# SSD mixer of a decoder trunk: decay exponents broadcast into two buffers a group ahead, selections as a job of their own, the state's product between the two diagonal parts

## The chip, the core and the metric

The kernel runs on one core of one Trainium2 chip. The metric is the device time of one execution in microseconds (us). Before the change three runs gave 1081.33, 1083.4 and 1087.55 us, a median of 1083.4.

## What is computed

A decoder trunk of two layers on 256 tokens of width 1024. Each layer is a half feed-forward block, a mixer and another half feed-forward block. The mixer of the first layer is attention, that of the second is a Mamba-2 SSD mixer, and this is the part that the change touches. Its 32 heads of width 64 fall into 4 groups of 8; each group has its own B and C (128 states), and the 256 tokens are two chunks of 128. Cut to what matters, per head of a group:

```
a_cs  = cumsum(dt * a)                               # within a chunk
decay = exp(a_cs[l] - a_cs[s])  for l >= s, else 0
y_diag = (C B^T * decay) @ (x * dt)                  # within a chunk
state  = B^T (x * dt * exp(a_cs[last] - a_cs))       # of the first chunk
y_off  = (C @ state) * exp(a_cs)                     # on the second chunk
y = (y_diag + y_off + d * x) * silu(z)
y = y * rsqrt(mean(y*y over the group) + eps) * norm ; out = y @ w_out
```

## The kernel before, in words

Weights are 128 x 1024 units in float32. `Weights.load` (L67) fetches a unit by the SP queue into one of RAW = 4 buffers, `ahead` (L75) splits it into a high part (cast on ScalarE, L86) and a low part (difference on VectorE, L87), PF = 4 units ahead of the one in use and into NB = 8 pairs of buffers. The projections use three matmuls per product for it: high by high, high by low, low by high (L253 to L255 and L258 to L260).

The mixer is `ssm` (L649). For each group g it projects a pair of columns (B and C of the group), two pairs (the group's x) and one z block, a `chunk` of 48 matmuls. `conv2` (L692) does the convolution and SiLU of a pair. The output projection `proj_out` (L300) follows, with 16 K tiles, four per group: 12 units of 24 matmuls, and then the last four (TAIL), taken together. These 96 matmuls all read `yh` and `yl` of group 3.

Everything else of a group is put between the projection's matmuls by a planner written by hand (L151 to L180). A job is a Python generator; each `yield` ends a step, and its value is a rest in us of the planner's own time before the next step is due. `tick(dt)` is called after every few matmuls: it moves that time on, lists the jobs whose predecessors have ended, in the order of their posting, and runs one step of those among the first WIN = 3 that are due. A job leaves the list only when the step after its last `yield` is asked for. `need(job)` runs all that is left of a job, and of what it depends on, at once.

```
ready = [g for g in bg if not any(d in bg for d in deps[g])]
for g in ready[:WIN]:
    if due[g] <= now[0]:
        step(g)
```

Jobs of the mixer: `dts` (L664) makes dt and the cumulated exponents, writes these to DRAM (`scr`, L680), rests L_DT = 18 and transposes them. `ssd(g)` (L710) is the group's scan. Its first step fetches the exponents of the group's 8 heads back from DRAM, broadcast to all 128 partitions: `sg` ("seg"), two transfers of 512 KB (L714), into a single buffer; GpSimd then fills the upper triangle with -BIG (`affine_select`, L716), and C B^T and B's transpose are made (L721, L722). Then come the transposes of x (L733) with `xd` (L737) and d * x on GpSimd (L738), the 16 exponentials (L746), `xe` (L753), the products of the decay with C B^T (L755), the state (L758) and its copy `sta` (L760), the two diagonal parts (L767, 32 matmuls each, added by VectorE in L769), and last the state's product with C (L772), which L774 and L776 scale and add. The banks for L758, L767 and L772 are two in all (`sbank`), taken in turns.

`gate(g, t)` (L780) multiplies by SiLU of z (L788), squares and sums on ScalarE (L790), takes the reciprocal root on GpSimd (L191, L194), scales on VectorE (L792), rests L_GATE = 7, transposes (L796) and splits into yh and yl (L184, L185). The transposes use the two banks of `tbank`, as do those of x.

What orders it: `ssd(g)` is posted after the pairs of group g with a rest of L_SD = 6, after `dts` and all earlier `ssd`; the two gates of g follow `ssd(g)`. Group g > 1 begins with `need(jobs[g - 2])`; before a z block's SiLU stands `need(*gates[g - 2])`; `before(i)` in the output projection calls `need` for the gates of group i // 4. The framework puts each engine's instructions into a fixed order when the kernel is built; it goes by the written order as the priority and may put an instruction that is ready ahead of one that is not.

Of the kernel before, what the change touches and what calls it, by code (L numbers as in the profile page):

```python
# [8 lines left out]
F32 = mybir.dt.float32  # L9
# [5 lines left out]
P = 128  # L15
# [14 lines left out]
WARM = 6  # L30
CONV = 0
L_HEAD, L_FG, L_SM, L_PT = 7.0, 20.0, 5.0, 2.5
L_DT, L_GATE, L_S0, L_S1, L_S2, L_S3, L_SD = 18.0, 7.0, 2.0, 6.0, 1.0, 2.0, 6.0
WIN = 3


# [66 lines left out]
def tile_trunk(ctx, tc, x, wp, sm, gains, ssm_norm, sinks, dskip, out):  # L103
# [18 lines left out]
    def tbank():  # L122
        return pt.tile([P, 512], F32, tag="tp", name="tp")
# [37 lines left out]
    def post(*gens, delay=0.0, after=()):  # L161
        for g in gens:
            due[g] = now[0] + delay
            deps[g] = after
            bg.append(g)
# [96 lines left out]
    def chunk(nk=2, nu=4):  # L262

        accs = [bank(), bank()]
        n = 1024 // nk
        for j in range(nu):
            wh, wl = W.take()
            for t in range(2):
                ts_ = slice(t * P, (t + 1) * P)
                for i in range(nk):  # L270
                    k = j * nk + i
                    ws = slice(i * n, (i + 1) * n)
                    mm_a(accs[t][:, 0:n], xh[:, k, ts_], xl[:, k, ts_], wh[:, ws], wl[:, ws],
                         k == 0, k == KT - 1)
                tick(1.3)
            W.free()
        return accs
# [371 lines left out]
    def ssm(nj, norm):  # L649
        with ExitStack() as es:  # L650
            sp = es.enter_context(tc.tile_pool(name="ssp", bufs=1, reuse_waits="tile"))
# [55 lines left out]

            y1, ngs = {}, {}

            def ssd(g, xT):  # L710
                hs = slice(g * 8, g * 8 + 8)
                sg = sp.tile([P, 2, 8, P], F32, tag="seg", name="seg", bufs=1)
                for c in range(2):
                    nc.sync.dma_start(sg[:, c], scr[None, hs, c * P : (c + 1) * P].partition_broadcast(P))  # L714
                for c in range(2):
                    G.affine_select(out=sg[:, c], in_=sg[:, c], pattern=[[0, 8], [1, P]],  # L716
                                    compare_op=ALU.is_ge, fill=-BIG, base=0, channel_multiplier=-1)
                b = tbank()
                for c in range(2):
                    cs = slice(c * P, (c + 1) * P)  # L720
                    T.matmul(b[:, cs], BT[:, g, cs], CT[:, g, cs], start=True, stop=True)  # L721
                T.transpose(b[:, 256:384], BT[:, g, 0:P], ident)  # L722
                cb = sp.tile([P, 2, P], F32, tag="cb", name="cb", bufs=2)
                A.copy(cb, b[:, 0:S].rearrange("p (c l) -> p c l", c=2))
                bn = sp.tile([P, P], F32, tag="bn", name="bn", bufs=2)
                A.copy(bn, b[:, 256:384])
                yield L_S0
                yt = sp.tile([P, 2, 8, HD], F32, tag="yb", name="y1", bufs=8)
# [30 lines left out]
                sta = sp.tile([P, 512], F32, tag="sta", name="sta", bufs=1)  # L759
                A.copy(sta, bs)  # L760
                yield L_S3
                for c in range(2):
                    b = sbank()
                    for q in range(8):
                        for e in range(2):
                            es_ = slice(e * 64, e * 64 + 64)
                            T.matmul(b[es_, q * HD : (q + 1) * HD], sg[:, c, q, es_], xd[c][:, q, :],  # L767
                                     start=True, stop=True)
                    V.tensor_tensor(yt[:, c], yt[:, c], b.rearrange("p (n d) -> p n d", n=8), ALU.add)  # L769
                    yield  # L770
                b = sbank()
                T.matmul(b, CT[:, g, P:S], sta, start=True, stop=True)  # L772
                tmp = sp.tile([P, 8, HD], F32, tag="xe", name="tmp", bufs=2)
                V.tensor_tensor(tmp, b.rearrange("p (n d) -> p n d", n=8),  # L774
                                eac[:, hs, None].broadcast_to([P, 8, HD]), ALU.mult)
                V.tensor_tensor(yt[:, 1], yt[:, 1], tmp, ALU.add)  # L776
                y1[g] = yt
                yield

# [27 lines left out]
                    r.append(s_)  # L807
                return r

            jobs, gates = [], []  # L810

            def pair(cts, dsts):
                conv2(pair_t(), cts, dsts)

            for g in range(4):
                if g > 1:
                    need(jobs[g - 2])
                xT = sp.tile([P, 4, S], F32, tag="xsT", name="xsT", bufs=2)
                bc = (16 + g, 20 + g), (BT[:, g, :], CT[:, g, :])
                if g == 0:  # L820

                    a0 = pair_t(True)
                    aj = small_proj(wdt)
                    tick(2.6)
                    a1 = pair_t()
                    need(nj)
                    conv2(a0, *bc)
                    jd = dts(aj)
                    post(jd)
                    conv2(a1, (0, 1), (xT[:, 0, :], xT[:, 1, :]))  # L830
                else:
                    pair(*bc)
                for q in range(2 if g == 0 else 0, 4, 2):
                    pair((g * 4 + q, g * 4 + q + 1), (xT[:, q, :], xT[:, q + 1, :]))
                jobs.append(ssd(g, xT))
                post(jobs[g], delay=L_SD, after=[jd] + jobs[:g])
                az = chunk()
                if g > 1:
                    need(*gates[g - 2])
                sz = silu_z(az)  # L840
                gates.append([gate(g, t, sz[t]) for t in range(2)])
                post(*gates[g], after=[jobs[g]])
# [124 lines left out]
```

## Time and profile before

| | us |
|---|---|
| median of three runs | 1083.4 (1081.33 to 1087.55) |
| the profiled execution | 1074.93 |
| its span | 1073.1 |
| TensorE busy | 1043.1 (97%) |
| VectorE busy | 808.7 (75%) |
| ScalarE busy | 621.0 (58%) |
| GpSimd busy | 99.4 (9%) |

The mixer lies between about 692 and 886 us of the span. The profile names engines PE (TensorE matmul), PEld (its weight load), DVE (VectorE), ACT (ScalarE), POOL (GpSimd) and SP (the queue that issues transfers). A matmul's end is modelled, so its recorded duration can reach into the next one's; where a wait begins and which instruction it is put down to is read from the waits. The granted clock is TensorE's, as a share of 2.4 GHz.

### The profile page before, as it was taken

The page shows a single profiled execution, that of the slowest core. Times are in us where ns is not written, and L with a number is a line of the kernel's source. Part 1 is how long each engine was busy: PE and PEld are TensorE (multiplying, and loading weights), DVE is VectorE, ACT ScalarE, POOL GpSimd, SP SyncE. Part 2 cuts the span into 40 slices and gives each one's busy share as a digit, 9 for nine tenths or more (in the row PEclk, how much of TensorE's full clock was granted, in tenths as well). Part 3 has the DMA queues.
Part 4 walks back from the last instruction along what each step waited for, and adds up shares of the span by engine and source line. Part 5 has one row for each costly group of instructions (what it writes and reads, how often), then busy time and mean ns, then how long its engine had stood idle before and what let it go on. Part 6 is the DMA issues. An engine that isn't in the chain of part 4 may idle for free.

```text
span 1073.1 us, 17287 instructions
## 1 busy us (share of the span) xinstructions
PE 1043.1 (97%) x6538; PEld 919.3 (86%) x6538; DVE 808.7 (75%) x1261; ACT 621.0 (58%) x1099; POOL 99.4 (9%) x117
## 2 busy tenths in 40 slices
PE   6999999997999999999999999999899999999998
PEld 5888888885888888888888888998888998888887
DVE  4898876666788888766888876587889768888751
ACT  5765654555666555454655654478878656555530
POOL 3000001243020000011000001101231121000000
PEclk8999999999999999999999999999999999999999
DMA  6776565534237666665666666534565636666550
GB/s 216 227 238 195 185 190 194 179 138 139 97 94 225 193 191 185 193 193 168 198 189 195 186 189 194 188 107 157 181 223 188 218 118 202 191 197 183 190 177 20
DMA packets 61603, 191.33 MB, mean 178 GB/s; under 512 B 6440, under 2 KB 15952, under 8 KB 61392
## 3 DMA queue, kind: packets, MB, share of 16 engines
q1 hardware_dynamic: 61520, 190.23, 56.5%
q8 instruction: 51, 0.84, 0.3%
q14 instruction: 32, 0.26, 0.1%
HBM read 189.12 MB, written 1.09 MB: 177 GB/s over the span
## 4 chain that ended last, share of the span: by engine, by line
PE 81%; DVE 5%; POOL 4%; ACT 3%; issue 3%; DMA 3%; SPq 0%; POOLq 0%; DVEq 0%; ACTq 0%
PE mm L339 44%; PE mm L340 23%; PE mm L258 3%; PE mm L260 3%; PE mm L259 3%; DMA seg<-scr_a 1%; DVE lo L87 1%; POOL rstd L194 1%; PE mm L253 1%; PE mm L254 1%; PE mm L255 1%; POOL sqa L216 1%; DVE cv L704 1%; ACT hi L86 1%; PE sb L767 1%
## 5 line engine op out<-in xcount | busy, mean ns | idle before, releaser
L86 ACT CAST hi<-raw 128x1024 fp32r<-128x1024 f32 (+1 forms) x350 | 362.6, 1041 | 346.9 <-PE mm L339 274.1
L87 DVE TENSOR_TENSOR lo<-raw,hi 128x1024 fp32r<-128x1024 f32 (+1 forms) x350 | 426.3, 1222 | 146.2 <-ACT hi L86 145.0
L339 PE MATMUL mm<-xhl,hi 128*128 128x512 f32 x1408 | 494.1, 395 | 7.2 <-ACT hi L86 4.9
L340 PE MATMUL mm<-xhl,lo 128*128 128x256 f32 x1408 | 395.9, 281 | 0.0
L339 PEld LDWEIGHTS mm<-xhl,hi 128*128 128x128 f32 x1408 | 265.6, 189 | 67.0 <-ACT hi L86 4.8
L340 PEld LDWEIGHTS mm<-xhl,lo 128*128 128x128 f32 x1408 | 268.3, 191 | 0.3 <-DVE lo L87 0.2
L339 PE MATMUL mm<-ht,hi 128*128 128x512 f32 x704 | 244.2, 392 | 0.0
L340 PE MATMUL mm<-ht,lo 128*128 128x256 f32 x704 | 197.0, 280 | 0.0
L339 PEld LDWEIGHTS mm<-ht,hi 128*128 128x128 f32 x704 | 131.8, 187 | 29.1
L340 PEld LDWEIGHTS mm<-ht,lo 128*128 128x128 f32 x704 | 133.2, 189 | 0.0
L216 POOL TENSOR_TENSOR sqa<-sqa,sqb 128x256 f32<-128x256 f32 x42 | 38.7, 921 | 597.0 <-ACT sqb L214 595.9
L253 PE MATMUL mm<-hi,xhl 128*128 128x512 f32 (+1 forms) x144 | 58.6, 407 | 0.0
L258 PE MATMUL mm<-xhl,hi 128*128 128x256 f32 x192 | 56.5, 294 | 0.0
L254 PE MATMUL mm<-lo,xhl 128*128 128x512 f32 (+1 forms) x144 | 55.5, 386 | 0.0
L255 PE MATMUL mm<-hi,xhl 128*128 128x512 f32 (+1 forms) x144 | 55.1, 383 | 0.0
L259 PE MATMUL mm<-xhl,hi 128*128 128x256 f32 x192 | 54.9, 286 | 0.0
L260 PE MATMUL mm<-xhl,lo 128*128 128x256 f32 x192 | 54.8, 285 | 0.0
L407 DVE SCALAR_TENSOR_TENSOR h<-mm,h 128x256 f32<-128x256 f32 x64 | 26.6, 422 | 36.5 <-PE mm L340 35.8
L206 DVE SCALAR_TENSOR_TENSOR xhl<-h,gn,xhl 128x256 fp32r<-128x256 f32 x48 | 35.8, 768 | 8.2 <-ACT xhl L205 8.2
L370 DVE TENSOR_TENSOR sumg<-sumg,rB 128x256 f32<-128x256 f32 x88 | 37.4, 425 | 4.9 <-ACT rB L237 2.3
L372 DVE TENSOR_TENSOR sumg<-sumg,rB 128x256 f32<-128x256 f32 x88 | 36.9, 419 | 4.4 <-ACT sumg L371 4.4
L377 DVE TENSOR_TENSOR sumu<-sumu,sumg 128x256 f32<-128x256 f32 x88 | 37.4, 425 | 2.6
(192 smaller groups left out, 1246.0 us busy)
## 6 DMA issues: line engine op xcount, KB each, us to landing
raw<-in_wp_dram SPq DMA_DIRECT2D x345, 512.0 KB, 3.6
seg<-scr_a SPq DMA_DIRECT2D x8, 512.0 KB, 7.0
fbc<-scr_f SPq DMA_DIRECT2D x1, 1024.0 KB, 5.7
ng<-in_ssm_norm_dram SPq DMA_DIRECT2D x4, 256.0 KB, 3.6
out_dram<-h SPq DMA_DIRECT2D x8, 128.0 KB, 2.7
h<-in_x_dram SPq DMA_DIRECT2D x3, 256.0 KB, 6.2
raw<-in_wp_dram SPq DMA_DIRECT2D x2, 256.0 KB, 2.7
smt<-in_sm_dram SPq DMA_DIRECT2D x1, 319.5 KB, 4.1
```

Of the source, the lines that this page charges most:

```text
L86: self.nc.scalar.copy(hi[:, cs], w[:, cs])
L87: self.nc.vector.tensor_tensor(lo[:, cs], w[:, cs], hi[:, cs].bitcast(F32), ALU.subtract)
L216: G.tensor_tensor(sqa, sqa, q, ALU.add)
L253: T.matmul(acc, sh, wh, start=start, stop=False)
L254: T.matmul(acc, sh, wl, start=False, stop=False)
L255: T.matmul(acc, sl_, wh, start=False, stop=stop)
L258: T.matmul(acc, wh, mh, start=start, stop=False)
L259: T.matmul(acc, wh, ml, start=False, stop=False)
L260: T.matmul(acc, wl, mh, start=False, stop=stop)
L339: T.matmul(acc, wh, mhl.rearrange("p e c -> p (e c)"), start=start, stop=False)
L340: T.matmul(acc[:, 0:S], wl, mhl[:, 0, :], start=False, stop=stop)
L370: V.tensor_tensor(s_, s_, rn[1], ALU.mult)
```

## The change

The broadcast and the selection leave `ssd` and become a job `seg(g)`: the first step issues the two transfers, rests L_SG = 9, the second does the two selections. `seg` has two buffers instead of one; `cb` and `bn` have one instead of two. `load_seg` posts the job of the next group: group 0's right after `dts`, group 1's after the z block of group 0 and after `dts` alone, group 2's after the first pair of group 1 and after `ssd(0)`, group 3's after the first pair of group 2 and after `ssd(0)` and `ssd(1)`. `ssd(g)` is now posted after `seg(g)` too. Within `ssd` the state's product moves between the two diagonal parts, with a rest of L_S4 = 2 on either side of it; before, the steps there followed each other without a rest.

```diff
--- before.py
+++ after.py
@@ -30,7 +30,7 @@
 WARM = 6
 CONV = 0
 L_HEAD, L_FG, L_SM, L_PT = 7.0, 20.0, 5.0, 2.5
-L_DT, L_GATE, L_S0, L_S1, L_S2, L_S3, L_SD = 18.0, 7.0, 2.0, 6.0, 1.0, 2.0, 6.0
+L_DT, L_GATE, L_S0, L_S1, L_S2, L_S3, L_S4, L_SD, L_SG = 18.0, 7.0, 2.0, 6.0, 1.0, 2.0, 2.0, 6.0, 9.0
 WIN = 3
 
 
@@ -707,22 +707,31 @@
 
             y1, ngs = {}, {}
 
-            def ssd(g, xT):
+            sgs = {}
+
+            def seg(g):
+
                 hs = slice(g * 8, g * 8 + 8)
-                sg = sp.tile([P, 2, 8, P], F32, tag="seg", name="seg", bufs=1)
+                sg = sgs[g] = sp.tile([P, 2, 8, P], F32, tag="seg", name="seg", bufs=2)
                 for c in range(2):
                     nc.sync.dma_start(sg[:, c], scr[None, hs, c * P : (c + 1) * P].partition_broadcast(P))
+                yield L_SG
                 for c in range(2):
                     G.affine_select(out=sg[:, c], in_=sg[:, c], pattern=[[0, 8], [1, P]],
                                     compare_op=ALU.is_ge, fill=-BIG, base=0, channel_multiplier=-1)
+                yield
+
+            def ssd(g, xT):
+                hs = slice(g * 8, g * 8 + 8)
+                sg = sgs.pop(g)
                 b = tbank()
                 for c in range(2):
                     cs = slice(c * P, (c + 1) * P)
                     T.matmul(b[:, cs], BT[:, g, cs], CT[:, g, cs], start=True, stop=True)
                 T.transpose(b[:, 256:384], BT[:, g, 0:P], ident)
-                cb = sp.tile([P, 2, P], F32, tag="cb", name="cb", bufs=2)
+                cb = sp.tile([P, 2, P], F32, tag="cb", name="cb", bufs=1)
                 A.copy(cb, b[:, 0:S].rearrange("p (c l) -> p c l", c=2))
-                bn = sp.tile([P, P], F32, tag="bn", name="bn", bufs=2)
+                bn = sp.tile([P, P], F32, tag="bn", name="bn", bufs=1)
                 A.copy(bn, b[:, 256:384])
                 yield L_S0
                 yt = sp.tile([P, 2, 8, HD], F32, tag="yb", name="y1", bufs=8)
@@ -759,7 +768,8 @@
                 sta = sp.tile([P, 512], F32, tag="sta", name="sta", bufs=1)
                 A.copy(sta, bs)
                 yield L_S3
-                for c in range(2):
+
+                def diag(c):
                     b = sbank()
                     for q in range(8):
                         for e in range(2):
@@ -767,13 +777,17 @@
                             T.matmul(b[es_, q * HD : (q + 1) * HD], sg[:, c, q, es_], xd[c][:, q, :],
                                      start=True, stop=True)
                     V.tensor_tensor(yt[:, c], yt[:, c], b.rearrange("p (n d) -> p n d", n=8), ALU.add)
-                    yield
+
+                diag(0)
+                yield L_S4
                 b = sbank()
                 T.matmul(b, CT[:, g, P:S], sta, start=True, stop=True)
                 tmp = sp.tile([P, 8, HD], F32, tag="xe", name="tmp", bufs=2)
                 V.tensor_tensor(tmp, b.rearrange("p (n d) -> p n d", n=8),
                                 eac[:, hs, None].broadcast_to([P, 8, HD]), ALU.mult)
                 V.tensor_tensor(yt[:, 1], yt[:, 1], tmp, ALU.add)
+                yield L_S4
+                diag(1)
                 y1[g] = yt
                 yield
 
@@ -807,7 +821,12 @@
                     r.append(s_)
                 return r
 
-            jobs, gates = [], []
+            jobs, gates, segs = [], [], []
+
+            def load_seg():
+                g = len(segs)
+                segs.append(seg(g))
+                post(segs[g], after=[jd] + jobs[: max(g - 1, 0)])
 
             def pair(cts, dsts):
                 conv2(pair_t(), cts, dsts)
@@ -827,14 +846,19 @@
                     conv2(a0, *bc)
                     jd = dts(aj)
                     post(jd)
+                    load_seg()
                     conv2(a1, (0, 1), (xT[:, 0, :], xT[:, 1, :]))
                 else:
                     pair(*bc)
+                    if g < 3:
+                        load_seg()
                 for q in range(2 if g == 0 else 0, 4, 2):
                     pair((g * 4 + q, g * 4 + q + 1), (xT[:, q, :], xT[:, q + 1, :]))
                 jobs.append(ssd(g, xT))
-                post(jobs[g], delay=L_SD, after=[jd] + jobs[:g])
+                post(jobs[g], delay=L_SD, after=[jd, segs[g]] + jobs[:g])
                 az = chunk()
+                if g == 0:
+                    load_seg()
                 if g > 1:
                     need(*gates[g - 2])
                 sz = silu_z(az)
```

## Rows read from the trace of the kernel before

**Rows 1.** The page, part 1: busy time, share of the span, instructions.

```profile
PE 1043.1 (97%) x6538; PEld 919.3 (86%) x6538; DVE 808.7 (75%) x1261; ACT 621.0 (58%) x1099; POOL 99.4 (9%) x117
```

**Rows 2.** Waits: TensorE from 100 us on, GpSimd in the mixer (sum, times, longest).

```profile
PE tp L490 <- DVE fq L514: 4.2, 1, 4.2
PE sb L772 <- DVE y L769: 2.8, 1, 2.8
PE tp L796 <- DVE xd L737: 2.2, 1, 2.2
...
POOL seg L716 <- DMA seg<-scr_a: 19.7, 6, 15.0
```

**Rows 3.** Stretches: length; busy PE, PEld, DVE, ACT, POOL; granted clock; DMA share; GB/s.

```profile
249.00:253.00 4.00, 4.00 (x20) 2.96 (x22) 2.08 (x2) 1.37 (x2) 0.00 (x0) 0.57 0.75 218
754.00:758.00 4.00, 4.00 (x20) 3.76 (x19) 4.00 (x6) 3.02 (x8) 0.00 (x0) 0.57 0.89 245
720.00:730.00 10.00, 9.82 (x83) 9.46 (x82) 6.26 (x10) 4.12 (x7) 1.74 (x2) 1.00 0.93 288
...
769.00:770.00 1.00, 1.00 (x10) 1.00 (x9) 1.00 (x2) 0.57 (x2) 0.00 (x0) 1.00 1.16 164
```

**Rows 4.** Timeline of TensorE, group 0 (start, us, engine, line, wait before).

```profile
746.78 1.15 PE L767 MATMUL sb<-xd,seg 128*64 128x64 f32 x32
...
753.41 0.70 PE L772 MATMUL sb<-sta,CT 128*128 128x512 f32 x1 [2.81 <-DVE y L769]
```

**Rows 5.** Timeline of VectorE and TensorE: first diagonal parts and their adds.

```profile
752.68 0.68 DVE L769 TENSOR_TENSOR y<-y,sb 128x512 f32<-128x512 f32 x1
...
784.37 1.15 PE L767 MATMUL sb<-xd,seg 128*64 128x64 f32 x32
...
786.15 0.68 DVE L769 TENSOR_TENSOR y<-y,sb 128x512 f32<-128x512 f32 x1
...
819.69 1.15 PE L767 MATMUL sb<-xd,seg 128*64 128x64 f32 x32
...
823.03 0.68 DVE L769 TENSOR_TENSOR y<-y,sb 128x512 f32<-128x512 f32 x1
```

**Rows 6.** Timeline of GpSimd and TensorE, 761 to 769 us.

```profile
761.90 1.55 POOL L716 TENSOR_SCALAR_AFFINE_SELECT seg<-seg 128x1024 f32<-128x1024 f32 x1 [0.47 <-DMA seg<-scr_a]
...
764.87 0.58 POOL L194 TENSOR_TENSOR rstd<-rstd,mhalf 128x1 f32<-128x1 f32 x1
...
768.79 0.44 PE L796 MATMUL tp<-ident,sz 128*128 128x128 f32 x2 [2.25 <-DVE xd L737]
```

**Rows 7.** Timeline of TensorE, group 3 in the output projection.

```profile
857.98 1.02 PE L772 MATMUL sb<-sta,CT 128*128 128x512 f32 x2
...
868.19 1.04 PE L796 MATMUL tp<-ident,sz 128*128 128x128 f32 x8
868.98 0.36 PE L258 MATMUL mm<-yh,hi 128*128 128x256 f32 x1
```

**Rows 8.** Timeline of VectorE and ScalarE, the last gate.

```profile
861.03 0.69 DVE L788 TENSOR_TENSOR y<-y,sz 128x512 f32<-128x512 f32 x1
862.20 1.23 DVE L87 TENSOR_TENSOR lo<-raw,hi 128x1024 fp32r<-128x1024 f32 x1 [0.48 <-ACT hi L86]
864.19 0.75 DVE L792 SCALAR_TENSOR_TENSOR sz<-y,rstd,ng 128x512 f32<-128x512 f32 x1 [0.77 <-POOL rstd L194]
...
868.82 1.08 ACT L184 CAST yh<-tp 128x512 fp32r<-128x512 f32 x2 [0.91 <-PE tp L796]
...
869.44 1.29 DVE L185 TENSOR_TENSOR yl<-tp,yh 128x512 fp32r<-128x512 f32 x2 [0.27 <-ACT yh L184]
```

**Rows 9.** Groups by line, 700 to 960 us (busy, mean ns, idle before).

```profile
L746 ACT ACTIVATE seg<-seg,nac 128x128 f32<-128x128 f32 x64 | 19.9, 392 | 2.1 <-POOL seg L716 2.0
...
L746 ACT ACT_TABLE_LOAD x5 | 6.4, 1283 | 0.1
```

**Rows 10.** The chain that ended last (start, us): group 3's state product.

```profile
858.14 0.86 PE sb L772 x2
```

## The prediction

> **What bounds the kernel now.** I read the page first: TensorE is busy for 97% of the span [rows 1]. So a change can win only what TensorE spends waiting or at the lower clock, and it loses as soon as it makes TensorE wait anew. Next the waits of TensorE alone, for the whole program after its start [rows 2]: of its three longest, two lie in the SSM mixer, 2.8 us before the product with the state (L772) and 2.2 us before transposes of the gate (L796). No wait of TensorE names the broadcast of the decay exponents; GpSimd waits for it, 19.7 us in all. The third view is the granted clock by stretches [rows 3]: in the 4 us that follow the 2.8 us wait it is 0.57 on average, at 1.2 GHz for most of them, and the same 0.57 follows the 4.2 us wait in the attention. Such a pause costs a further 4 x 0.43 = 1.7 us. After the pause of 2.2 us the clock stayed at 1.00, so this price does not always fall due. All that this mixer can give back is therefore 2.8 + 1.7 + 2.25 = 6.8 us, 0.6% of the time.
>
> Where the two waits come from. After the second diagonal part of group 0 TensorE stands for 2.81 us, until 753.41 [rows 4]. The product with the state takes the PSUM bank of the first diagonal part, which was done at 747.9 (746.78 + 1.15 [rows 4]); VectorE adds it only at 752.68, 4.8 us later [rows 5]: VectorE is behind. In groups 1 and 2 that lag is 0.6 us (785.5 to 786.15) and 2.2 us (820.8 to 823.03) [rows 5]. The second wait begins on GpSimd: a select waits for the broadcast and ends at 763.45, the reciprocal root of the gate stands behind it until 765.45, VectorE's L792 waits for that, and behind L792 the product that would empty the bank for the transposes at 768.79 [rows 6].
>
> **The change, part by part.** No matmul, cast or activation is added or removed, so TensorE's work stays the same and the sum is of waits only. It stands on the order in which the hand-written planner puts the steps; I replayed that order with the kernel's own figures (5.2 for a pair of columns, 10.4 for a z block, 2.6 for a unit of the output projection, the L_ constants, at most WIN = 3 ready jobs a tick). The replay of the kernel before puts 78 matmuls between the last state product and the last eight transposes; the trace has the two at 858 and 868 us, in that order [rows 7].
>
> (1) *The jobs start later.* For group 0 the broadcast goes out at the same tick as before (33.15 of the planner's time), but the job now waits for the selection job, which rests L_SG = 9.0: it starts at 43.55 instead of 33.15. From group 1 on another thing delays it. When one job ends, the ready list is gate t=0, gate t=1, next selection, next job: the job is fourth, WIN lets three through, and the gates hold their places for L_GATE = 7.0. Group 1 starts at 63.7 instead of 55.25, group 2 at 89.7 instead of 80.6, group 3 at 116.35 instead of 106.6. The matmuls of the projections are where they were; the job's steps move back by 8 to 10.
>
> (2) *The end of the mixer.* Before, the last job ended at 128.7, the gates of group 3 at 137.15, and the last four K tiles began at 137.8. After, the last job has reached only its first diagonal part at 136.5. At 137.8 `before(12)` calls `need(*gates[3])`, and that forces out state product, second diagonal part, both gates and their eight transposes in one go. Behind them on TensorE stand the 96 matmuls of the tail, and all read group 3's yh and yl: nothing can fill the wait. Its length, from the end of the second diagonal part: the add 0.73 (its row 0.68 [rows 5] and a hand-over), then L788's start to L792's end, 861.03 to 864.94 = 3.9 [rows 8], then one half of the transposes, casts and differences: 0.63 to the first cast, 0.54 for it, 0.65 for its difference, with hand-overs 1.9 [rows 7, 8]; in all, with 0.1 between, 6.65. Of it 0.8 are the transposes, which stood on TensorE before too (868.19 to 868.98 [rows 7]). That leaves 5.9 us of standing. The clock after it: 1.7, as after the two shorter pauses of rows 3. Together **+7.6**. Bounds: 5.0 (the differences partly covered, no fall of the clock) and 10.1 (two L87 of 1.23 in the way on VectorE [rows 8]). I take 7.6, nearest to the rows of this very chain.
>
> (3) *The end of group 0's job.* Before, `need(jobs[0])` at the end of group 1's z block forced out one step, the state product; now five: the second masking product, state, diagonal part, state product, diagonal part. In the new order the state product takes the bank of the state, free early, and its 0.86 us [rows 10] cover part of the add's lag; but the second diagonal part then waits for that add. With 0.8 for the add and its hand-overs the wait is lag + 0.8 - 0.86: with lag 4.8 it is 4.7, and 6.4 with the clock's 1.7; with 2.2 it is 2.1, with 0.6 it is 0.5; against 4.5 before. Besides, the 16 exponentials (0.31 us apart, 0.39 each [rows 9]) now stand 24 matmuls ahead of the forced end, 5.2 of the planner's time, and 4.9 + 1.3 (table load [rows 9]) + 0.7 (L753, a product as large as the add) may leave 1.7 uncovered. Between ends of -4.5 (wait gone) and +3.6 I take **0**, nearest to the large lag, which is this group's own row: the wait moves from the state product to the second diagonal part.
>
> (4) *The end of group 1's job* is now forced in the same way at the end of group 2's z block, where TensorE had no wait: +0.5 with the lag of group 1's row, up to 2.1 with group 2's, 0 if VectorE is prompt. I take **+0.5**. Group 2's job ends inside the output projection with 24 matmuls between its steps: 0.
>
> (5) *The gate's transposes in group 1.* The gate's roots come ahead of the next selects on GpSimd now, and the job's transposes after the gate's: that wait goes, **-2.25** (other end 0).
>
> (6) *Queues.* On SP the broadcasts of groups 0 and 1 go out together: 1 MB more ahead of the weights, at the 288 GB/s of that stretch 3.6 us [rows 3]. Weights are split four units ahead; a unit is 24 matmuls and 83 ran in those 10 us, so four units last 11.6 us: hidden, and 3.6 if that cover were gone. Group 2's load must still wait for the last diagonal part of group 0 and holds up the weight loads behind it, hidden by the same four units. On GpSimd the selects (1.55 us [rows 6]) run while it idles. `cb` and `bn` in one buffer: the next job starts only after the last one ended; 0.
>
> By rows 2 the earlier load is worth no more than the 2.25 of (5). The Trainium skill (Trainium Kernel Development and Optimization, Best Practices) says to double-buffer so that DMA overlaps compute; by that rule the second buffer should bring a gain, and the sum would be that of the first rival.
>
> Sum: 7.6 + 0 + 0.5 - 2.25 = **+5.85 us**. The profiled execution took 1074.93 us, which would become 1080.8; it lies 8.5 below the median of the runs, 1083.4, to which I add the same difference: 1089.2. About 0.5%, or 5.4 us, is what a measurement of this kernel can tell from no change.
>
> **Rivals.**
> *A. The loads ahead free the whole mixer (not slower).* Place: the chain of select, exponentials, mask and products. If its steps run as soon as their data is there, whatever the planner's due times, the late start costs nothing, the tail stays fed and both waits go: -4.5 - 2.25 = -6.75, 1076.6. It decides by where group 3's second diagonal part runs: 7 us or more before the tail. For it: VectorE's order is not strictly the written one (L792 of one gate at 864, after an L87 of a later weight [rows 8]). Against it: TensorE's is, in what I checked [rows 7]. The double-buffering rule ends here. 0.12.
> *B. Tail exposed, but the new order does cure the first wait:* 7.6 + 0.5 - 2.25 - 4.5 = +1.35, 1084.8. For it: lags of 0.6 and 2.2 in the other groups [rows 5]; against: 4.8 in this one. 0.24.
> *C. The forced ends are worse:* exponentials late in group 0, lag 2.2 in group 1: 7.6 + 3.6 + 2.1 - 2.25 = +11.1, 1094.5. For it: ScalarE and VectorE carry the weight splits there too. Against: exponentials may go ahead of their place. 0.17.
> *D. The change doesn't move what counts* (the load was hidden, the tail is absorbed): 0, 1083.4. 0.05.
> My forecast has 0.42.
>
> **How the numbers follow.** The forecast is the likeliest case, 1089.2. Low end: tail 5.0, first wait gone, 2.25 won: -1.75, rounded to 1081. High end: C with the tail at 10.1 is +13.6, and a part of the 2.25 not won makes it 1098. A lies outside. Slower by over 0.5%: all of C, a little over half of the forecast's 0.42, and a trace of B, 0.44. Within: the rest of these and D, 0.42. Faster: A and the low edge of B, 0.14.
>
> **What would show it.** Right: a new wait of TensorE of 5 to 7 us at the last transposes (L796), ahead of the last K tiles near 870 us, then some 4 us at a clock near 0.57; the broadcasts of groups 0 and 1 together near 720; selects of later groups long before their exponentials; the wait at 766 gone. Wrong: TensorE busy without a break from 850 to 880, or the second diagonal part of group 3 done well before the tail.

## The result, and the profile after

Four runs of each kernel gave a median of 1098.07 us after the change (1089.89 to 1100.9) against 1084.56 before (1081.33 to 1087.55): a ratio of 1.011, 95% interval 1.0065 to 1.0156. Repeated later with six and 23 runs (experiment 1), it was 1093.94 against 1078.05, 1.0131 (1.0107 to 1.0156). The change makes the kernel slower, by 12 to 14 us going by the ratios; the medians lie 13.5 and 15.9 apart.

The profiled execution after took 1099.08 us, its span 1097.1, where that of before had 1074.93 and 1073.1. The mixer, from the transposes of dt (L685 in both listings) to those of the norm that follows (L233), takes 188.4 us (723.08 to 911.48) against 170.6 (720.12 to 890.68): 17.8 more. The rest of the 24 lies where the code is the same. In the profiles of this study L685 begins anywhere from 719.28 to 724.42, whichever kernel it is, so a difference ahead of the mixer is not taken for the change's.

Page, part 1, of the kernel after; beside [rows 1] the same number of instructions on every engine but ScalarE, which has 12 more:

```profile
PE 1055.8 (96%) x6538; PEld 923.5 (84%) x6538; DVE 813.0 (74%) x1261; ACT 637.1 (58%) x1111; POOL 99.0 (9%) x117
```

Waits of TensorE from 100 us on, after (line, releaser: sum, times, longest). L810 are the gate's transposes (L796 before), L767 makes the state (L758), L742 are the transposes of x (L733):

```profile
PE tp L810 <- DVE sz L806: 9.9, 4, 3.0
...
PE sb L767 <- DVE xe L762: 2.7, 1, 2.7
PE tp L742 <- ACT bn L735: 2.1, 1, 2.1
```

Of [rows 2] the attention's wait (L490) is as before, 4.1 us. The two of the mixer, 2.8 and 2.2 us, are replaced by 9.9, 2.7 and 2.1.

**The tail.** Timeline of TensorE, after, at the end of group 3 (L784 is the state's product with C, L777 the second diagonal part, L258 the first matmul of the last four K tiles):

```profile
879.09 1.02 PE L784 MATMUL sb<-sta,CT 128*128 128x512 f32 x2
880.04 1.15 PE L777 MATMUL sb<-xd,seg 128*64 128x64 f32 x32
883.84 1.12 PE L810 MATMUL tp<-ident,sz 128*128 128x128 f32 x4 [2.65 <-DVE sz L806]
888.00 1.12 PE L810 MATMUL tp<-ident,sz 128*128 128x128 f32 x4 [3.04 <-DVE sz L806]
889.79 1.22 PE L258 MATMUL mm<-yh,hi 128*128 128x256 f32 x4 [0.68 <-ACT yh L184]
```

State product, diagonal part, gates and tail follow each other with nothing of the projection between them, as the replay of the planner had them. From the diagonal part's end (880.04 + 1.15 = 881.2) to the tail are 8.6 us, in which TensorE only transposes. Before, 78 matmuls lay between the last step and the last transposes [rows 7]. VectorE, after, in the same stretch:

```profile
880.75 1.22 DVE L87 TENSOR_TENSOR lo<-raw,hi 128x1024 fp32r<-128x1024 f32 x1
881.89 0.69 DVE L788 TENSOR_TENSOR y<-y,tmp 128x512 f32<-128x512 f32 x1
883.03 0.75 DVE L806 SCALAR_TENSOR_TENSOR sz<-y,rstd,ng 128x512 f32<-128x512 f32 x1 [0.46 <-POOL rstd L194]
883.70 0.68 DVE L779 TENSOR_TENSOR y<-y,sb 128x512 f32<-128x512 f32 x1
...
887.19 0.75 DVE L806 SCALAR_TENSOR_TENSOR sz<-y,rstd,ng 128x512 f32<-128x512 f32 x1 [0.89 <-POOL rstd L194]
```

The add of the diagonal part (L779) begins only at 883.70, 2.5 us after its product's end: ahead of it stand a weight's difference (L87), the add of the state's product (L788) and the scaling of the other chunk's gate (L806), which waited for its root.

Stretches, after (length; busy PE, PEld, DVE, ACT, POOL; granted clock; DMA share; GB/s):

```profile
757.00:763.00 6.00, 5.64 (x42) 4.26 (x43) 4.67 (x6) 5.55 (x7) 0.00 (x0) 0.50 0.34 104
...
815.00:818.00 3.00, 3.00 (x16) 3.00 (x16) 3.00 (x6) 2.00 (x3) 0.00 (x0) 0.50 0.27 77
...
889.00:893.00 4.00, 3.33 (x16) 3.21 (x16) 0.69 (x1) 0.59 (x1) 0.00 (x0) 0.50 0.00 0
```

TensorE ran at 1.2 GHz behind three of its new waits: in group 0, behind the gate of group 1, and as the tail began.

**Group 0.** Timeline of TensorE, after:

```profile
744.66 0.66 PE L742 MATMUL tp<-ident,xsT 128*128 128x128 f32 x4 [2.15 <-ACT bn L735]
...
757.36 2.07 PE L767 MATMUL sb<-xe,bn 128*128 128x512 f32 x2 [2.72 <-DVE xe L762]
```

The state waits for `xe`, which takes its factor from the exponentials (L755). ScalarE's timeline says why they are late:

```profile
747.46 1.28 ACT L755 ACT_TABLE_LOAD   x1
748.75 0.40 ACT L755 ACTIVATE seg<-seg,nac 128x128 f32<-128x128 f32 x1
749.17 1.28 ACT L706 ACT_TABLE_LOAD   x1
750.47 0.42 ACT L706 ACTIVATE xsT<-cv 128x256 f32<-128x256 f32 x1
750.79 0.57 ACT L744 COPY y<-tp 128x512 f32<-128x512 f32 x1
751.38 1.28 ACT L755 ACT_TABLE_LOAD   x1
752.67 3.91 ACT L755 ACTIVATE seg<-seg,nac 128x128 f32<-128x128 f32 x13
```

One exponential slips in between two SiLUs (L706) and pays two table loads, and the same happened at 740.75; a first one had run at 733.32. The other 13 run only from 752.67 on, 2 us before TensorE reaches the state (757.36 - 2.72 = 754.64). Groups by line, after, 700 to 960 us:

```profile
L755 ACT ACT_TABLE_LOAD x11 | 14.1, 1283 | 0.2
...
L706 ACT ACT_TABLE_LOAD x10 | 12.8, 1283 | 2.7 <-DVE cv L704 2.5
```

Before, the exponentials loaded their table five times [rows 9]. The 12 more instructions of ScalarE on the page are table loads.

**The gates of groups 0 and 1.** Timeline of GpSimd and TensorE, after, in group 1; another such wait, of 1.41 us, ended at 775.76:

```profile
808.79 1.09 POOL L720 TENSOR_SCALAR_AFFINE_SELECT seg<-seg 128x1024 f32<-128x1024 f32 x1 [2.93 <-DMA seg<-scr_a]
809.97 1.07 POOL L191 TENSOR_SCALAR rstd<-gss 128x1 f32<-128x1 f32 x1
811.12 0.57 POOL L194 TENSOR_TENSOR rstd<-rstd,mhalf 128x1 f32<-128x1 f32 x1
...
813.34 0.66 PE L810 MATMUL tp<-ident,sz 128*128 128x128 f32 x4 [2.77 <-DVE sz L806]
```

The first gate's root is ahead of the select, the second gate's is behind it again, as in [rows 6]: the select waits for its broadcast and the root for the select.

### The profile page after: what moved, and what is told of

Its sections match the earlier page's. It is cut to its first block, busy times and chain, and to the rows that moved or that the text cites. A ratio compares the mean times of both kernels' runs of the same rounds, so it can differ in the third digit from the quotient of the medians.

```text
span 1097.1 us, 17295 instructions
## 1 busy us (share of the span) xinstructions
PE 1055.8 (96%) x6538; PEld 923.5 (84%) x6538; DVE 813.0 (74%) x1261; ACT 637.1 (58%) x1111; POOL 99.0 (9%) x117
## 4 chain that ended last, share of the span: by engine, by line
PE 76%; DVE 7%; ACT 6%; POOL 4%; issue 3%; DMA 3%; SPq 0%; POOLq 0%; ACTq 0%; DVEq 0%
PE mm L339 43%; PE mm L340 22%; PE mm L258 2%; DVE cv L704 2%; PE mm L259 2%; PE mm L260 2%; DVE lo L87 1%; ACT hi L86 1%; POOL rstd L194 1%; ACT seg L755 1%; DMA seg<-scr_a 1%; POOL sqa L216 1%; DMA raw<-in_wp_dram 1%; PE mm L254 1%; POOL rstd L191 1%
## 5 line engine op out<-in xcount | busy, mean ns | idle before, releaser
L87 DVE TENSOR_TENSOR lo<-raw,hi 128x1024 fp32r<-128x1024 f32 (+1 forms) x350 | 425.0, 1219 | 154.6 <-ACT hi L86 153.4
L258 PE MATMUL mm<-xhl,hi 128*128 128x256 f32 x192 | 57.6, 300 | 0.0
L253 PE MATMUL mm<-hi,xhl 128*128 128x512 f32 (+1 forms) x144 | 56.1, 390 | 0.1
L255 PE MATMUL mm<-hi,xhl 128*128 128x512 f32 (+1 forms) x144 | 54.9, 381 | 0.0
L704 DVE SCALAR_TENSOR_TENSOR cv<-cvx,smt,cv 128x255 f32<-128x255 f32 (+2 forms) x72 | 36.7, 558 | 4.3 <-ACT cv L701 4.1
```

The costliest lines, as they stand in the source:

```text
L87: self.nc.vector.tensor_tensor(lo[:, cs], w[:, cs], hi[:, cs].bitcast(F32), ALU.subtract)
L253: T.matmul(acc, sh, wh, start=start, stop=False)
L255: T.matmul(acc, sl_, wh, start=False, stop=stop)
L258: T.matmul(acc, wh, mh, start=start, stop=False)
L704: V.scalar_tensor_tensor(o_[:, d_:S], a_[:, 0 : S - d_], cw[:, 3 - d_ : 4 - d_], o_[:, d_:S], ALU.mult, ALU.add)
```

## Experiments

Two theories stood against each other. **Late steps** (theory A of the expectations): the planner starts the jobs later (fourth in a window of three, and the new rests), so that their ends are forced where TensorE has nothing else. **Table loads** (theory B): the late start is absorbed, and what costs is the 12 loads and the ScalarE time around them. A third, theory C, was that the double burst of broadcasts holds up the weights. Every ratio is to the kernel before, run in turn on the same chip, where its median was 1077.87, 1079.72, 1078.05 or 1078.0 us. No kernel leaves out a part of the computation. In the expectations e1, e5 and e7 are experiments 2, 4 and 9.

**1. The change again.** No edit.

> The changed kernel itself, on the same chip and in the same rounds as the two beside it. Its first measurement was a ratio of 1.011 with an interval of 0.9 per cent width. Sum of the prediction 1.0055; the pauses read from its trace add to more, about 17 us longer in the mixer, 1.013 to 1.016.

Measured: 1093.94 us, 1.0131 (1.0107 to 1.0156). In the profile the mixer's stretch (L685 to L233) is 187.8 us; the waits are those of the first profile, 9.9 us at L810 among them, but for L742, which has 2.7 where the first had 2.1.

**2. No late start.** After, with both rests at 0 and the selection jobs outside the window's count:

```diff
-        for g in ready[:WIN]:
+        for g in [g for g in ready if g in free] + [g for g in ready if g not in free][:WIN]:
...
                 segs.append(seg(g))
+                free.append(segs[g])
...
-L_S4, L_SD, L_SG = 2.0, 6.0, 9.0
+L_S4, L_SD, L_SG = 0.0, 6.0, 0.0
```

> The changed kernel with only its waiting taken out: the selection jobs don't count among the three of the planner's window, L_SG = 0 and L_S4 = 0. Two buffers, the loads ahead and the new order stay. By the planner's figures group 3's last steps are back 90 matmuls before the tail. Theory A (the late start and the forced ends cost the time): the wait of TensorE before the last K tiles (8.6 us from the second diagonal part to the first tail matmul) is gone, no pause over 3 us is left, 1076 to 1086 us, no slower than before. Theory B (early exponentials between SiLUs cost table loads on ScalarE: 33 loads in the program instead of 21): this kernel has 31, so it stays 5 to 10 us slower than before, about 1090 to 1096. Theory C (the double burst of broadcasts holds up the weights): also slower, with waits of TensorE on weight splits near 735 to 745 us.

Measured: 1079.51 us, 1.0013 (0.9994 to 1.0032). Timeline of TensorE at its end:

```profile
863.93 1.15 PE L777 MATMUL sb<-xd,seg 128*64 128x64 f32 x32
...
874.47 1.04 PE L810 MATMUL tp<-ident,sz 128*128 128x128 f32 x8
```

The last transposes come 9.4 us after the diagonal part, and no wait stands between them and the tail. The exponentials still load their table ten times (ScalarE 633.3 us busy, 637.1 in the change). The four broadcasts still go out in a row, from 723.14 on. So the loss goes with the late steps while the loads and the burst stay: that speaks for the first theory and against the other two. What is left of the change, two buffers filled ahead and the new order, is worth nothing that five rounds show.

**3. Exponentials behind the copies.** After, with the first exponential of a group ordered behind the copy of y on ScalarE, so that it can't slip between SiLUs:

```diff
-                    A.copy(yt[:, c], bv)
+                    ycopy = A.copy(yt[:, c], bv)
...
-                i = None
+                i = ycopy
```

> The changed kernel, late starts and all, with only the exponentials held behind the copies of y: 23 table loads instead of 33. Theory A: the pause at the tail stays at 7 to 9 us, the time 1090 to 1099 as for the change, at most 4 us less from group 0's job. Theory B: most of the 13 us come back, 1084 to 1088, and the tail is short.

Measured: 1093.48 us, 1.015 (1.0127 to 1.0173). Only six loads at L755 and six at L706 are left, ScalarE's busy time falls to 624.1 us, and the ratio is no lower than that of the change. Waits of TensorE in the mixer:

```profile
PE tp L810 <- DVE sz L806: 10.1, 4, 3.0
PE sb L767 <- DVE xe L762: 4.8, 1, 4.8
```

The tail is unchanged. In group 0 the wait of 2.1 us for `bn` is gone and the one for `xe` has grown from 2.7 to 4.8: the sum is the same. All 16 exponentials now run in a row behind one load. ScalarE's timeline:

```profile
751.16 4.78 ACT L755 ACTIVATE seg<-seg,nac 128x128 f32<-128x128 f32 x16
```

They end 32.3 us after the transposes of dt (L685, 723.62), where those of the change end after 33.5: no later, but TensorE, not held up at the transposes of x, comes earlier and stands at the state instead. The mixer's stretch is 185.6 us in this profile, 2 to 3 less than in those of the change, but fewer loads alone save nothing that these four runs show.

**4. Both.** Experiment 2 with the edit of experiment 3.

> As e1, and the first exponential of a group is issued on ScalarE only behind the copy of the second half of y (L744), so that none slips ahead between SiLUs: 19 table loads in the program. Theory A: like e1, within 3 us of it, 1076 to 1084. Theory B: 5 to 10 us faster than e1 and level with before or better. Theory C: as slow as e1.

Measured: 1078.86 us, 1.0005 (0.9989 to 1.0021). Against experiment 2 no difference shows. Its longest wait stands at 770.61:

```profile
PE tp L810 <- DVE xd L746: 3.3, 1, 3.3
```

**5. The tail alone.** The kernel *before*, with group 3's job alone put off:

```diff
-                post(jobs[g], delay=L_SD, after=[jd] + jobs[:g])
+                post(jobs[g], delay=20.0 if g == 3 else L_SD, after=[jd] + jobs[:g])
```

> The kernel before with one number changed: group 3's job rests 20 instead of 6, so that it starts where the changed kernel starts it, and its last steps are forced out ahead of the last K tiles. Nothing else of the change is in it. Theory A: TensorE stands 6 to 9 us at the last transposes, then runs some 4 us at the half clock; 8 to 11 us slower than before. Theory B or C: no more than 4 us slower, since neither table loads nor bursts are added.

Measured: 1086.95 us, 1.009 (1.007 to 1.011). Timeline of TensorE, and the stretch behind it:

```profile
882.84 1.12 PE L796 MATMUL tp<-ident,sz 128*128 128x128 f32 x4 [5.38 <-DVE sz L792]
884.63 1.22 PE L258 MATMUL mm<-yh,hi 128*128 128x256 f32 x4 [0.68 <-ACT yh L184]
```
```profile
885.00:889.00 4.00, 4.00 (x20) 4.00 (x20) 0.30 (x1) 0.00 (x0) 0.00 (x0) 0.50 0.00 0
```

One late job, with nothing else of the change, makes the tail's wait and its half clock and costs 0.9% of 1077.87, 9.7 us (7.5 to 11.9 by the interval; the medians lie 9.1 apart). The profiled execution is the slowest of the six, 1091.14 us.

**6. The order alone.** The kernel *before* (here L767 is a diagonal part), with the state's product between the diagonal parts and a plain `yield` between the steps:

```diff
-                for c in range(2):
+                def diag(c):
...
+                diag(0)
+                yield
...
+                yield
+                diag(1)
```

> The kernel before with the new order of the group's last steps alone (diagonal part, state's product, diagonal part), no rests, one buffer for the exponents. Term (3) of the prediction: the wait of 2.8 us moves from the state's product to the second diagonal part and keeps its size, 1076 to 1080 us against 1077.9. Rival B: the new order cures it, that wait is under 1 us and 3 to 5 us are gained, 1073 to 1075.

Measured: 1077.87 us, 0.9984 (0.9963 to 1.0004). Of the waits in the mixer, the longest:

```profile
PE sb L767 <- DVE y L769: 2.6, 1, 2.6
```

That is the 2.8 us of [rows 4], now ahead of the second diagonal part.

**7. A window of four.** After, with all rests kept:

```diff
-WIN = 3
+WIN = 4
```

> The changed kernel with WIN = 4 and nothing else: the selection job no longer keeps the next scan out of the window, the rests L_SG = 9 and L_S4 = 2 stay. By the planner's figures group 3's second diagonal part comes back to 42 matmuls before the tail, but the gate's transposes are still forced out just ahead of it. If the window is what made the tail late, the pause there falls from 7 to 8 us to 2 to 3, and the time is 1081 to 1087, some 7 to 11 below the change. If the rests alone made it late, 1088 or more.

Measured: 1087.36 us, 1.0081 (1.0055 to 1.0106). At the tail only 1.2 and 0.7 us are left, as the first case had it, though the time is just above its range. The longest waits that remain are in group 0, at its second gate and at its state:

```profile
PE tp L810 <- DVE sz L806: 4.2, 1, 4.2
PE sb L767 <- DVE xe L762: 2.7, 1, 2.7
```

**8. No rests.** After, with the window of three kept:

```diff
-L_S4, L_SD, L_SG = 2.0, 6.0, 9.0
+L_S4, L_SD, L_SG = 0.0, 6.0, 0.0
```

> The changed kernel with L_SG = 0 and L_S4 = 0 and the window left at three: only the starvation by the window is left. By the planner's figures group 1 starts 3 us late instead of 8, group 3's second diagonal part is 78 matmuls before the tail, and only the gate's transposes are forced out ahead of it. If the rests carry the loss: 1082 to 1085 with 2 to 3 us of waiting at the tail. If the window carries it whatever the rests: 1088 or more.

Measured: 1083.43 us, 1.0047 (1.0023 to 1.0071). Waits of TensorE in the mixer:

```profile
PE tp L810 <- DVE xd L746: 6.5, 4, 2.6
PE sb L784 <- ACT sta L769: 2.2, 1, 2.2
```

At the tail 1.2 and 0.7 us are left here too. Either repair takes most of the tail's wait and neither takes the whole loss; experiment 2, which does away with the rests and with the window's hold on the selection jobs, does.

**9. Selects behind the roots, with nothing late.** Experiment 4, and the selects of groups 2 and 3 ordered on GpSimd behind the second gate's root of two groups before:

```diff
+                with tc.issue_after(roots[g - 2].ins) if g > 1 else nullcontext():
...
                 r = rstd_of(ssq, 1)
+                roots[g] = last_root[0]
```

The selection job rests 4.0 there for groups 2 and 3.

> e5 (no late start, exponentials behind the copy) with the selections of groups 2 and 3 issued on GpSimd only behind the second root of the gate of the group two before. In e5 that root stood behind a selection that waited for its broadcast, and TensorE waited 3.3 us for it at the gate's transposes. Theory: that wait goes, with the half clock behind it 3 to 5 us, 1073 to 1076 us, below the kernel before. If something else delays the transposes there: as e5, 1078 to 1080.

Measured: 1076.69 us, 0.9977 (0.9957 to 0.9997). The wait of experiment 4 is down to 1.1 us:

```profile
PE sb L787 <- ACT sta L772: 1.7, 1, 1.7
...
PE tp L814 <- DVE xd L749: 1.1, 1, 1.1
```

The best of the list, by 0.23% or 2.5 us, with an interval that ends just below 1: hardly to be told from no change, and just above the 1073 to 1076 that the theory asked for.

**10. Selects behind the roots, in the change itself.** After with the edit of experiment 9 alone, all rests and the window kept.

> The changed kernel with one addition: the selects of groups 2 and 3 stand on GpSimd behind the second gate's reciprocal root of the group two before, as term (5) of the prediction had taken for granted. All late starts and rests are kept. Theory (the select ahead of the root is what makes the gate's transposes wait in groups 0 and 1): the waits of 1.41 and 2.77 us at L810 in the stretch 770 to 816 shrink to 0 to 1 us each, the half clock behind the second (1.7 us) goes; the tail's 2.65 and 3.04 stay. 3 to 6 us less than the change itself, 1.008 to 1.011 of before where the change has 1.0131. Rival (VectorE is late there whatever GpSimd does, the root is only the last of several): L810 still waits 1 us or more in both places, and the ratio stays at 1.012 to 1.015. Second rival (the selects now come late and hold the exponentials): a new wait at L767 or L777 in groups 2 and 3.

Measured: 1095.47 us, 1.015 (1.0116 to 1.0184). Timeline of TensorE:

```profile
773.80 0.66 PE L814 MATMUL tp<-ident,sz 128*128 128x128 f32 x4 [1.54 <-DVE sz L810]
...
808.56 0.66 PE L814 MATMUL tp<-ident,sz 128*128 128x128 f32 x4 [0.44 <-DVE sz L810]
...
814.38 0.71 PE L733 MATMUL tp<-CT,BT 128*128 128x128 f32 x4 [1.58 <-DVE yl L185]
```

Timelines of VectorE and GpSimd, group 0:

```profile
772.18 1.56 DVE L810 SCALAR_TENSOR_TENSOR sz<-y,rstd,ng 128x512 f32<-128x512 f32 x1 [1.00 <-POOL rstd L196]
...
772.11 2.59 POOL L723 TENSOR_SCALAR_AFFINE_SELECT seg<-seg 128x1024 f32<-128x1024 f32 x2
```

In group 1 the wait of 2.77 us is down to 0.44, but 1.58 come back at the next transposes in the same banks (L733). In group 0 it stays, 1.54 where it was 1.41, although no select is ahead of the root any more. The root is done at 772.15 where it was done at 774.92, but TensorE also arrives earlier, at 772.26 instead of 774.35, and the scaling (L810), with the selects now right beside it, takes 1.56 us where it took 0.75. The gate's square on ScalarE (770.45) comes behind VectorE's product at 768.97 in a queue of adds. So the select was the cause in group 1; how much of group 0's wait was due to it this run does not settle. The mixer's stretch is 184.8 us in the profile, 3 less than in experiment 1, but the time of the six runs shows no gain.

**11. A third buffer for x.** Experiment 6, with three buffers of `xsT` and `need(jobs[g - 3])`, so that no job is forced at the end of a z block of groups 1 and 2.

```diff
-                if g > 1:
-                    need(jobs[g - 2])
-                xT = sp.tile([P, 4, S], F32, tag="xsT", name="xsT", bufs=2)
+                if g > 2:
+                    need(jobs[g - 3])
+                xT = sp.tile([P, 4, S], F32, tag="xsT", name="xsT", bufs=3)
```

> The kernel before with the new order, no rests, and a third buffer for a group's x, so that group 0's last steps are not forced out at the start of group 2 but keep 6 matmuls between them. Theory (the forced end is what makes VectorE's lag felt): the wait of 2.8 us and the half clock behind it are gone, 1072 to 1075 us. If the lag of VectorE is felt anyway: 1076 to 1080, like the order alone.

Measured: 1080.38 us, 1.0015 (0.9995 to 1.0036). A miss: with matmuls between the steps TensorE still waits.

```profile
PE tp L800 <- DVE xd L737: 5.0, 2, 3.1
PE sb L767 <- DVE y L769: 3.0, 2, 2.3
```

So the forced end is not the only reason for group 0's wait; VectorE's lag is felt with six matmuls between the steps as well.

**12. State first.** Experiment 9, with the copy `sta` and the diagonal adds put ahead:

```diff
-                A.copy(sta, bs)
+                with tc.high_priority(offset=HIGH):
+                    A.copy(sta, bs)
...
-                    V.tensor_tensor(yt[:, c], yt[:, c], b.rearrange("p (n d) -> p n d", n=8), ALU.add)
+                    with tc.high_priority(offset=HIGH):
+                        V.tensor_tensor(yt[:, c], yt[:, c], b.rearrange("p (n d) -> p n d", n=8), ALU.add)
```

> e7 (no late start, exponentials behind the copy, selections behind the roots) with the copy of the state and the adds of the diagonal parts given a high priority when the engines' orders are fixed. In e7 TensorE still waits 1.7 us for that copy and 0.8 us for the adds. Theory: both waits go, 2 to 3 us, 0.995 of the kernel before. If VectorE's and ScalarE's total load there sets the pace, the time moves to other waits: as e7, 0.997 to 1.000.

Measured: 1077.04 us, 0.9985 (0.9966 to 1.0004). A second miss: the wait for `sta` falls from 1.7 to 0.8 us, but that for the adds is 1.1 instead of 0.8, and the gate's transposes wait 2.6 where they waited 1.1. That fits the other reading, that moving one wait brings the next where VectorE and ScalarE have much to do; the run does not show more than that.

## Why the prediction came out as it did

The direction held and the mechanism that it put first is the one that the runs confirm. The size was short: +5.85 us forecast, 12 to 14 measured, more than twice as much. The median of 1098.07 stands at the very top of the range, and that the range reached so far was luck: its upper end came from rival C, whose cost for group 1 did not come, while the gates, for which the range held nothing worse than no gain, cost 3.4 us. Of the signs, the pause at the last transposes (2.65 + 3.04), the low clock behind it and the double broadcast came; the wait at 766 did not go.

**Terms (1) and (2), the late start and the tail: right, the tail undersized.** The trace has the order of the replay: group 3's job begins 90 matmuls of the output projection later than before, which at 2.6 a unit of 24 is 9.75 of the planner's time (116.35 less 106.6). Experiments 2 and 5 show both halves: without the lateness there is no loss, and lateness of group 3 alone costs 9 to 10 us. In the profile the tail is 8.6 of standing, less the 0.8 of transposes that stood there before, and half of the 3.2 us from 889.8 to 893: 9.4, for 7.6 predicted and inside the bounds of 5.0 and 10.1. The step that was short is "the add 0.73", taken as beginning at the diagonal part's end. It began 2.5 us later, behind a weight's difference and, for the most part, behind the add of the state's product and the first gate's scaling, which the same forced end had pushed there. The rest of the chain was 0.6 us shorter than priced: the first matmul of the tail waits for the cast alone, and the difference counted at 0.65 runs beside it.

**Term (3), group 0's forced end: wrong.** I took 0 and had 3.6 as the upper end. The profile shows 2.15 + 2.72 and half of the 5.6 us from 757.4 to 763, 7.7 in all; before it was 4.5. So +3.2. The order itself did what I said: experiment 6 moves the wait and changes no time. In the change it does not even appear at the second diagonal part, ahead of which the build put 16 matmuls of the next pair. What came in its place is what I had as the bound, the exponentials ahead of the forced end, at 1.7 us. The timeline suggests the extra table loads as the reason; experiment 3 says no: with one load and no single exponentials TensorE stands 4.83 us, as long as the 2.15 + 2.72 here. The step that failed is the cover. I had let the exponentials begin 24 matmuls, 5.2 of the planner's time, ahead of the forced end; in experiment 3 they began 0.7 us before TensorE came to the state (751.16 against 751.90), behind casts, SiLUs and copies on ScalarE.

**Term (4), group 1's end: the number by luck.** Predicted was +0.5, the second diagonal part waiting for the first one's add; measured is 0.59, but elsewhere. Timeline of TensorE, after:

```profile
793.96 0.50 PE L254 MATMUL mm<-lo,xhl 128*128 128x512 f32 x1 [0.59 <-DVE lo L87]
```

It is a weight's low part, which VectorE makes late behind the mask product of the late job (L764). The add itself began 3.1 us after its product (797.64 to 800.72), more than the 0.6 and 2.2 that I had taken, and TensorE did not feel it, since the build had put 24 matmuls of group 3's first pair ahead of the state's product with C.

**Term (5), the gate's transposes: wrong.** "The gate's roots come ahead of the next selects" held for the first gate of a group only. I had read that order from the planner; the second root is still behind the select in both groups, and the waits add to 1.41 + 2.77 and half of the 3 us at the lower clock: 5.7, for 2.25 before. So +3.4 in place of -2.25, the largest error of the sum. Experiment 10 shows that even with that order granted a wait stays in group 0 and part of group 1's comes back at the next transposes. And the chain read from [rows 6] was not the select's alone. Timeline of GpSimd, before, between that select and the root:

```profile
763.43 1.04 POOL L738 TENSOR_TENSOR y<-y,db 128x512 f32<-128x512 f32 x1
```

The product of the scan stands there too, and VectorE's L792 then took 1.52 us, twice its usual 0.75. So a select out of the way need not have given back all of the 2.25.

**Term (6), the queues: right as far as the trace shows.** The broadcasts of groups 0 and 1 went out together, four transfers in a row. Timeline of SP's queue, after:

```profile
722.99 7.06 SPq L717 DMA_DIRECT2D seg<-scr_a  x4
```

The only new wait for a weight is that of term (4), for a difference on VectorE and not for a transfer.

With the measured sizes the sum is 9.4 + 3.2 + 0.6 + 3.4 = 16.6 of the 17.8 us of the mixer in the profiles. The low clock outlasts the three windows shown by 0.3 to 0.6 us each, which would add some 0.7 in all. The runs give 12 to 14 by the ratios. Part of the difference is that one execution of before stands for many: its 1074.93 us lie near the low end of the kernel's runs (1073.77 to 1087.55 over all comparisons). I had taken that gap for a constant 8.5; against the later medians of 1078 to 1079.7 it is 3 to 5.

**The rivals.** A, the loads ahead freeing the mixer, needs the last diagonal part done 7 us ahead of the tail. Experiment 2 has it there, yet of its gain nothing came: the two waits of [rows 2] give way to others, 2.2 us for the copy of the state (L784) the longest. The Trainium skill (Trainium Kernel Development and Optimization, Best Practices) advises double buffering to overlap DMA with compute; by 1.0013 (0.9994 to 1.0032) the second buffer brings nothing here that shows. B fell with experiment 6, in which the new order left 2.6 of the 2.8 us standing. C has the size, but of its terms beyond the forecast only group 0's came. D fell with the result.

**Still open.** How the loss divides between the tail and the rest. The tail alone costs 9.7 us in the kernel before; the change without most of its tail wait keeps 8.7 us in experiment 7 and 5.1 in experiment 8, where 14 less 9.7 would leave 4.3. With intervals of 2 to 3 us to either side on each of these, the runs do not show whether the parts add up. No run takes the late start out of group 0 alone, so its 3.2 us are read from the profile.

## What to carry to other kernels

In a list planned by hand, a new job takes a place in the window: count who is let through at each tick, and replay the order to the last consumer before judging what a prefetch brings. Price a forced end with the queue of every engine in its chain at that moment, not with the bare durations; here the add began 2.5 us later than priced. And where the order on an engine decides a term, take it from the order that the build writes, not from the planner's, or give the term both signs.

## What the runs showed of the hardware

A lone exponential between SiLUs costs two table loads of 1283 ns on ScalarE; the change had 23 loads at L755, L706 and L820 in the mixer where before had 11, five of them in [rows 9]. The Trainium skill (ScalarE: Activation LUTs, Table sets: the hidden batching unit) says to group activations by table set; its section What ACT_TABLE_LOAD costs gives 1283 ns for a load and some 1380 ns of drain beside it. The load agrees to the nanosecond; the rows show no such drain: the copy that ends at 751.36 is followed by a load at 751.38 and the first exponential at 752.67. And grouping them (experiments 3 and 4) gained nothing that the runs show; ScalarE was busy for 58% of the span.

TensorE's clock did not answer every pause in the same way. The wait of 2.72 us in group 0 was followed by 0.50 from 757 to 763; in the profile of experiment 1, the same kernel with the same wait (2.72, until 757.90), the low clock ended at 761:

```profile
757.00:763.00 6.00, 5.10 (x47) 3.77 (x48) 5.15 (x6) 5.97 (x9) 0.00 (x0) 0.72 0.26 73
```

In experiment 7 a wait of 2.74 at the same instruction (757.99) was followed by 1.00 up to 762. In the prediction I had charged 1.7 us where the clock falls. These profiles hold about 1.5 to 3, and none in that case.

VectorE's scaling of the gate takes 0.75 us in 89 of its 112 executions in the 14 profiles and 1.52 to 1.65 us in the other 23, as in experiment 10 at 772.18. In each of the 23 a select or the product of d and x had begun on GpSimd at that moment, in most 0.07 us before it. Where GpSimd's began 0.14 us or more behind it, the scaling kept its 0.75. No run varied this by itself. For a gate's chain it means that what stands behind the root on GpSimd can cost VectorE 0.8 us.
